# A decoder trunk's down-projection in seven block products instead of eight

## The chip, the core and the metric

The kernel runs on one core of a Trainium2 chip. Its engines work side by side: TensorE (PE, with its weight loads PEld), VectorE (DVE), ScalarE (ACT), GpSimd (POOL) and SyncE (SP), which only issues DMAs here. The metric is the device time of one execution in microseconds. The profile is one execution on the same chip; line numbers such as L650 are lines of the kernel before.

## The reference

One layer over 1024 tokens of 1024 channels, all float32:

```python
h = rms_norm(x, norm_mix_g); z = h @ w_in              # 1024 -> 2048
x = x + concat([pooling(z), diff_attention(z)]) @ w_out
h = rms_norm(x, norm_ffn_g)
gu = h @ ffn_w_in                                      # 1024 -> 2 * 2816
g = causal_depthwise_conv(gu[..., :2816])              # width 3
x = x + (silu(g) * gu[..., 2816:]) @ ffn_w_out         # 2816 -> 1024, the down-projection
return rms_norm(x, norm_final_g)
```

## The kernel before

Every large product is made from float32r parts: an operand is split into a high part (a cast on ACT) and a low part (the difference, on DVE or POOL), and one block takes three matmuls, high by high, high by low and low by high. `split` and `psplit` do it (L78 to L84), `mm3` issues the three.

The stages follow one another. In-projection, attention and pooling (L321 to L511); the output projection in three groups (`out_rows`, L530); then `norm2` and `pair_blocks` (L561 to L600) normalise the rows and build seven transposed operands, b11, b21, b22 and t1 to t4, with high and low parts in 14 buffers of the pool h2. t1 to t4 are sums and differences of row tiles; those of the last pair are made on DVE. The up loop (L689) runs over 22 channel tiles. For each, `up_weights` loads two raw tiles ru and rg (two buffers, tag rw), forms sums sa and sb on POOL and DVE and the high and low parts (uh and ul, sah and sal, and so on), one tile ahead; `ffn_up` makes seven products of 12 matmuls, gathers them in g and cv, applies the convolution, SiLU and gate, and stores cv as 128 rows of `act_rows` in DRAM.

The down-projection (L754) takes the 22 channel tiles in groups of 3, 3, 3, 3, 3, 3 and 4. A group loads and splits its activations (`pair_of`, the low part on DVE) and weights (the low part on POOL). `ffn_down` (L740) goes over 8 row tiles and two column halves: a PSUM bank gets the 9 (or 12) matmuls of the group, and DVE adds it to the row xr of the residual (L750). In the last group `finish` follows each row tile: squares on ACT, a square root, three Newton steps on DVE, the product with the norm's weights, the store.

Instructions are put in order by a scheduler when the program is built; a pool with several buffers makes a new tile wait until the old one in that buffer was last read. Each engine then works in the order given, and so does the SP queue.

## Time and profile before

| | us |
|---|---|
| three runs | 1113.57 to 1114.74, median 1114.7 |
| the profiled execution | 1115.49 |
| its span, first to last instruction | 1113.7 |
| first and last matmul of the down-projection | 857.6 and 1105.8 |

The span is what the trace covers; the profiled execution's own time holds another 1.8 us around it. The up loop's steady part is looked at from 500 to 820, the down-projection's from 885 to 1105.

### The profile page before, as it was taken

How to read it: one execution, taken by the hardware profiler on the slowest of the kernel's cores; microseconds unless marked ns; L12 is line 12 of the kernel's file. 1: busy time of each engine (PE TensorE's matmuls, PEld its weight loads, DVE VectorE, ACT ScalarE, POOL GpSimd, SP SyncE). 2: the span in 40 equal slices, each digit the busy share in tenths (PEclk: the TensorE clock that was granted, in tenths of full speed). 3: DMA queues.
4: the chain of work that ended last, by engine and by line, in shares of the span. 5: the costliest groups of instructions: out<-in, count | busy, mean ns of one | idle time of the engine just before them, and what ended most of it. 6: DMA issues, size and time to landing. Idle time of an engine off the chain costs nothing.

```text
span 1113.7 us, 13597 instructions
## 1 busy us (share of the span) xinstructions
PE 1066.6 (96%) x5011; PEld 884.0 (79%) x5011; DVE 732.3 (66%) x1213; ACT 475.9 (43%) x775; POOL 341.7 (31%) x240
## 2 busy tenths in 40 slices
PE   5999999999899997999999999999999999999997
PEld 4988888887677675878888888888888788888885
DVE  7556787877797689577657656755665655544545
ACT  5557476655752355244333443443344222111133
POOL 3232242433730247133312232221314322221211
PEclk9999999999899998999999999999999999999999
DMA  8010110110386742123122212222247632212112
GB/s 242 28 50 27 43 46 19 43 39 26 133 278 216 242 171 76 57 95 95 57 94 95 93 59 96 90 81 76 82 127 267 223 114 99 89 60 95 39 50 102
DMA packets 85990, 111.76 MB, mean 100 GB/s; under 512 B 3618, under 2 KB 66303, under 8 KB 85924
## 3 DMA queue, kind: packets, MB, share of 16 engines
q1 hardware_dynamic: 79300, 86.78, 24.4%
q10 hardware_dynamic: 6624, 24.12, 5.5%
q8 instruction: 39, 0.64, 0.2%
q14 instruction: 27, 0.22, 0.1%
HBM read 82.57 MB, written 28.32 MB: 100 GB/s over the span
## 4 chain that ended last, share of the span: by engine, by line
PE 81%; DVE 8%; issue 4%; DMA 3%; ACT 1%; POOL 1%; SPq 1%; DVEq 0%; ACTq 0%; POOLq 0%
PE p L650 36%; PE fo L747 7%; PE fo L749 7%; PE fo L748 7%; PE tpa L402 1%; PE z_q L144 1%; PE z_q L145 1%; PE z_q L143 1%; PE o L538 1%; PE o L539 1%; PE o L540 1%; PE z_p L143 1%; PE z_p L144 1%; PE z_p L145 1%; PE z_v L143 1%
## 5 line engine op out<-in xcount | busy, mean ns | idle before, releaser
L747 PE MATMUL fo<-w,a 128*128 128x512 f32 x352 | 137.3, 390 | 2.8 <-DVE xr L750 2.8
L750 DVE TENSOR_TENSOR xr<-xr,fo 128x512 f32<-128x512 f32 x112 | 75.9, 684 | 97.0 <-PE fo L749 96.3
L748 PE MATMUL fo<-w,a 128*128 128x512 f32 x352 | 137.0, 389 | 0.0
L749 PE MATMUL fo<-w,a 128*128 128x512 f32 x352 | 137.0, 389 | 0.0
L80 POOL TENSOR_TENSOR w<-rw,w 128x1024 fp32r<-128x1024 f32 x22 | 61.3, 2796 | 156.4 <-ACT w L79 151.1
L628 POOL TENSOR_TENSOR sa<-rg 128x512 f32<-128x512 f32 x22 | 32.9, 1495 | 209.8 <-DMA rg<-in_ffn_w_in_dram 201.3
L80 POOL TENSOR_TENSOR ul<-ru,uh 128x1024 fp32r<-128x1024 f32 x22 | 58.1, 2642 | 71.8 <-PE p L650 37.6
L747 PEld LDWEIGHTS fo<-w,a 128*128 128x128 f32 x352 | 66.1, 188 | 17.6 <-DVE xr L750 4.0
L749 PEld LDWEIGHTS fo<-w,a 128*128 128x128 f32 x352 | 66.1, 188 | 13.9
L748 PEld LDWEIGHTS fo<-w,a 128*128 128x128 f32 x352 | 66.1, 188 | 13.6
L79 ACT CAST a<-ra 128x1024 fp32r<-128x1024 f32 x22 | 23.1, 1051 | 118.8 <-DVE xr L750 64.1
L362 ACT ACTIVATE p<-p,nm 128x128 f32<-128x128 f32 (+7 forms) x64 | 49.6, 776 | 40.9 <-DVE nm L361 40.5
L650 PE MATMUL p<-t4h,gt 128*128 128x512 f32 x176 | 58.9, 396 | 1.7 <-DVE g L675 1.7
L629 DVE TENSOR_TENSOR sa<-sa,ru 128x512 f32<-128x512 f32 x22 | 39.9, 1814 | 21.1 <-POOL sa L628 21.1
L538 PE MATMUL o<-woh,yh 128*128 128x512 f32 x128 | 51.9, 409 | 1.6 <-DVE x L541 1.4
L349 POOL CAST qz<-q 64x128 fp32r<-64x128 f32 x64 | 24.5, 384 | 92.3 <-PE s L353 85.4
L79 ACT CAST uh<-ru 128x1024 fp32r<-128x1024 f32 x22 | 23.2, 1054 | 68.0 <-PE p L650 67.4
L539 PE MATMUL o<-wol,yh 128*128 128x512 f32 x128 | 50.6, 397 | 1.4 <-POOL wol L80 1.4
L677 DVE TENSOR_TENSOR g<-eb,p 128x512 f32<-128x512 f32 x22 | 15.1, 687 | 55.5 <-PE p L650 55.5
L80 DVE TENSOR_TENSOR a<-ra,a 128x1024 fp32r<-128x1024 f32 x22 | 43.0, 1956 | 12.1 <-ACT a L79 11.6
L540 PE MATMUL o<-woh,yl 128*128 128x512 f32 x128 | 50.0, 393 | 0.9 <-DVE yl L80 0.9
L79 ACT CAST gt<-rg 128x512 fp32r<-128x512 f32 x22 | 13.7, 623 | 82.1 <-PE p L650 75.1
(264 smaller groups left out, 3111.0 us busy)
## 6 DMA issues: line engine op xcount, KB each, us to landing
x_rows<-x ACTq DMA_DIRECT2D x24, 512.0 KB, 3.6
ru<-in_ffn_w_in_dram SPq DMA_DIRECT2D x22, 512.0 KB, 4.0
rg<-in_ffn_w_in_dram SPq DMA_DIRECT2D x22, 512.0 KB, 3.9
act_rows<-cv ACTq DMA_DIRECT2D x22, 512.0 KB, 2.6
rw<-in_ffn_w_out_dram SPq DMA_DIRECT2D x22, 512.0 KB, 4.4
ra<-act_rows SPq DMA_DIRECT2D x22, 512.0 KB, 3.4
x<-in_x_dram SPq DMA_DIRECT2D x16, 512.0 KB, 5.6
x<-x_rows SPq DMA_DIRECT2D x16, 512.0 KB, 3.7
```

Of the source, the lines that this page charges most:

```text
L79: nc.scalar.copy(hi, src)
L80: (lo_eng or nc.gpsimd).tensor_tensor(lo, src, hi.bitcast(F32), op=ALU.subtract)
L362: nc.scalar.activation(s[:, 0:w], s[:, 0:w], AF.Exp, bias=negm[:, c:c + 1], accum_out=sums[:, c:c + 1])
L538: nc.tensor.matmul(ps, yh[:, ts], wh[:, cs], start=n == 0, stop=False)
L539: nc.tensor.matmul(ps, yh[:, ts], wl[:, cs], start=False, stop=False)
L540: nc.tensor.matmul(ps, yl[:, ts], wh[:, cs], start=False, stop=n == len(wo) - 1)
L629: nc.vector.tensor_tensor(s2, s1, a11, op=ALU.subtract)
L650: nc.tensor.matmul(ps, w[:, k, :], h[:, k, :], start=start and k == 0 and n == 0, stop=k == 3 and n == 2, skip_group_check=not start)
L747: nc.tensor.matmul(ps, ah[:, ts], wh[:, cs], start=n == 0, stop=False)
L748: nc.tensor.matmul(ps, ah[:, ts], wl[:, cs], start=False, stop=False)
L749: nc.tensor.matmul(ps, al[:, ts], wh[:, cs], start=False, stop=n == len(ops) - 1)
L750: nc.vector.tensor_tensor(xr[t][:, cs], xr[t][:, cs], ps, op=ALU.add)
```

## The change

The down-projection is made from seven products (Strassen's scheme in Winograd's form) instead of eight. Tokens are cut into halves, channel tiles into even and odd ones, output columns into halves. A product takes 512 tokens, 11 channel pairs and 512 columns, and keeps one PSUM bank for each of its four row tiles over all channels: 4 x 11 x 3 = 132 matmuls. Its banks are then added to one to four blocks of the residual (`ADDS`, `add_product`).

- The seven activation operands are made in the up loop: after each odd tile `store_act` stores three blocks of cv as they are and four sums of two tiles, which POOL forms (sm). `act_rows` becomes seven arrays.
- The weights stay in SBUF as four quarters x, y, z, v of float32 (`load_quarter`, three buffers of h2 each, `wx0` to `wv2`). Four products need differences of quarters; DVE writes them in place (`operands`, L755 of the kernel after).
- Each product goes through six steps of two channel pairs (the last has one). A step loads one activation block, splits it (ah, al) and splits the weights (bh and bl, or b); `al5_2` is product 5, channel pair 2. The order of the products is 1, 2, 5, 7, 6, 3, 4.
- In the last product the top four row tiles are finished beside it; its last three steps are held back and run row tile by row tile.
- In `up_weights` of the second tile a column of the last normalised row is copied into ru and rg before they are loaded.
- cv has three buffers, two small pads are put among the constants, the DMA scratch is 2048.

```diff
-DOWN = [3] * 6 + [4]
+DOWN = (("1", "x", None), ("2", "z", None), ("5", "x", "yx"), ("7", "y", "vy"), ("6", "x", "vx"), ("3", "v", None),
+        ("4", "z", "xz"))
+ADDS = {"1": ((0, 0), (0, 1), (1, 0), (1, 1)), "2": ((0, 0),), "3": ((0, 1),), "4": ((1, 0),), "5": ((0, 1), (1, 1)),
+        "6": ((0, 1), (1, 0), (1, 1)), "7": ((1, 0), (1, 1))}
+STEPS = ((0, 2), (2, 2), (4, 2), (6, 2), (8, 2), (10, 1))
+SCRATCH = 2048
...
+PADS = (8, 8)
...
-    act_d = nc.dram_tensor("act_rows", (FF, S), F32).ap()
+    act_d = nc.dram_tensor("act_rows", (7, FF // 2, 512), F32).ap()
...
+    const.tile([P, PADS[0]], F32, name="pad0")
...
+    const.tile([P, PADS[1]], F32, name="pad1")
...
-        ta = mid.tile([P, S], F32, tag="cv", bufs=2, name=f"ta{j}")
-        tb = mid.tile([P, S], F32, tag="cv", bufs=2, name=f"tb{j}")
+        ta = mid.tile([P, S], F32, tag="cv", bufs=3, name=f"ta{j}")
+        tb = mid.tile([P, S], F32, tag="cv", bufs=3, name=f"tb{j}")
...
+            if ct == 1:
+                nc.vector.tensor_copy(r[:, 0:1], x1[NT - 1][:, D - 1:D])
...
-        cv = mid.tile([P, S], F32, tag="cv", bufs=2, name=f"cv{ct}")
+        cv = cvs[ct] = mid.tile([P, S], F32, tag="cv", bufs=3, name=f"cv{ct}")
...
-        nc.scalar.dma_start(act_d[ct * P:(ct + 1) * P, :], cv)
+        store_act(ct, cv)
+    cvs = {}
+    def op_rows(n, m, count=1):
+        return act_d[n - 1, m * P:(m + count) * P, :].rearrange("(m p) c -> p m c", p=P)
+    def store_act(ct, cv):
+        m = ct // 2
+        if ct % 2 == 0:
+            nc.scalar.dma_start(act_d[0, m * P:(m + 1) * P, :], cv[:, 0:512])
+            return
+        for i, n in enumerate((2, 4)):
+            nc.scalar.dma_start(act_d[n - 1, m * P:(m + 1) * P, :], cv[:, i * 512:i * 512 + 512])
+        a11, a21, a12, a22 = cvs[ct - 1][:, 0:512], cvs[ct - 1][:, 512:1024], cv[:, 0:512], cv[:, 512:1024]
+        sm = [mid.tile([P, S], F32, tag="sm", bufs=2, name=f"sm{m}_{i}") for i in range(2)]
+        s1, s2, s3, s4 = [sm[i // 2][:, (i % 2) * 512:(i % 2) * 512 + 512] for i in range(4)]
+        nc.gpsimd.tensor_tensor(s3, a11, a21, op=ALU.subtract)
+        nc.gpsimd.tensor_tensor(s1, a21, a22, op=ALU.add)
+        nc.gpsimd.tensor_tensor(s2, s1, a11, op=ALU.subtract)
+        nc.gpsimd.tensor_tensor(s4, a12, s2, op=ALU.subtract)
+        for n, t in ((5, s1), (6, s2), (7, s3), (3, s4)):
+            nc.sync.dma_start(act_d[n - 1, m * P:(m + 1) * P, :], t)
...
+    wq = {}
+    def load_quarter(q):
+        b, cs = dict(x=(0, 0), y=(0, 1), z=(1, 0), v=(1, 1))[q]
+        src = ffn_w_out.rearrange("(m b p) c -> b p m c", b=2, p=P)[b][:, :, cs * 512:cs * 512 + 512]
+        wq[q] = [h2.tile([P, 4, 512], F32, tag="h2", name=f"w{q}{i}") for i in range(3)]
+        for m, n in STEPS:
+            nc.sync.dma_start(wq[q][m // 4][:, m % 4:m % 4 + n, :], src[:, m:m + n, :])
+    def quarter(q, m, n):
+        return wq[q][m // 4][:, m % 4:m % 4 + n, :]
+    def operands(gi, m, n):
+        num, q, upd = DOWN[gi]
+        if upd:
+            a, b = upd
+            if q == b:
+                nc.vector.tensor_tensor(quarter(b, m, n), quarter(a, m, n), quarter(b, m, n), op=ALU.subtract)
+        raw = mid.tile([P, 2, 512], F32, tag="rw", bufs=2, name=f"ra{num}_{m}")[:, 0:n, :]
+        nc.sync.dma_start(raw, op_rows(int(num), m, n))
+        if gi == 0:
+            a2 = h2.tile([P, 4, 512], F32R, tag="h2", name=f"a{num}_{m}")
+            ah, al = a2[:, 0:n, :], a2[:, 2:2 + n, :]
+        else:
+            ah = wide.tile([P, 2, 512], F32R, tag="x", bufs=4, name=f"ah{num}_{m}")[:, 0:n, :]
+            al = mid.tile([P, 2, 512], F32R, tag="cv", bufs=3, name=f"al{num}_{m}")[:, 0:n, :]
+        split(ah, al, raw, nc.vector)
+        if m // 2 % 2:
+            b2 = h2.tile([P, 4, 512], F32R, tag="h2", name=f"b{num}_{m}")
+            wh, wl = b2[:, 0:n, :], b2[:, 2:2 + n, :]
+        else:
+            wh = mid.tile([P, 2, 512], F32R, tag="st", bufs=2, name=f"bh{num}_{m}")[:, 0:n, :]
+            pool, tag, bufs = (mid, "sm", 2) if gi else (wide, "x", 4)
+            wl = pool.tile([P, 2, 512], F32R, tag=tag, bufs=bufs, name=f"bl{num}_{m}")[:, 0:n, :]
+        split(wh, wl, quarter(q, m, n))
+        return ah, al, wh, wl
+    def banks(gi):
+        if gi % 2:
+            return [sc_ps(f"fo_{gi}_{j}") for j in range(3)] + [mm_ps(f"fo_{gi}_3")]
+        return ([tp_ps(f"fo_{gi}_{j}").rearrange("p a b -> p (a b)") for j in range(2)]
+                + [mm_ps(f"fo_{gi}_2"), pv_ps(f"fo_{gi}_3")])
+    def tile_part(ps, op, j, m, n):
+        ah, al, wh, wl = op
+        js = slice(j * P, (j + 1) * P)
+        for i in range(n):
+            mm3(ps, ah[:, i, js], al[:, i, js], wh[:, i, :], wl[:, i, :], m + i == 0, m + i == NCT // 2 - 1)
+    def add_product(num, j, ps):
+        for h, c in ADDS[num]:
+            t, cs = 4 * h + j, slice(c * 512, c * 512 + 512)
+            if num == "4":
+                nc.vector.tensor_tensor(xr[t][:, cs], xr[t][:, cs], ps, op=ALU.subtract)
+            else:
+                nc.vector.tensor_tensor(xr[t][:, cs], xr[t][:, cs], ps, op=ALU.add)
+    outs, sums = {}, {}
+    def half_sum(t, half):
+        if t not in outs:
+            outs[t] = h2.tile([P, 4, 512], F32, tag="h2", name=f"o_{t}").rearrange("p a c -> p (a c)")[:, 0:D]
+            sums[t] = small.tile([P, 2], F32, tag="fs", bufs=8, name=f"ss2_{t}")
+        nc.scalar.activation(outs[t][:, 0:512], xr[t][:, half * 512:half * 512 + 512], AF.Square,
+                             accum_out=sums[t][:, half:half + 1])
...
-        if pool_path:
-            nc.scalar.mul(o, xg, r)
+        nc.scalar.mul(o[:, 512:1024], o[:, 512:1024], r)
+        nc.vector.scalar_tensor_tensor(o[:, 0:512], xr[t][:, 0:512], r, g_bc3[:, 0:512], op0=ALU.mult, op1=ALU.mult)
...
+        nc.scalar.dma_start(out[t * P:(t + 1) * P, 512:1024], o[:, 512:1024])
+        nc.sync.dma_start(out[t * P:(t + 1) * P, 0:512], o[:, 0:512])
+    def right_half(t):
+        half_sum(t, 1)
+        nc.gpsimd.tensor_tensor(outs[t][:, 512:1024], xr[t][:, 512:1024], g_bc3[:, 512:1024], op=ALU.mult)
...
+    late = 3
+    for gi, (num, q, upd) in enumerate(DOWN):
+        for c in (q if upd is None else upd):
+            if c not in wq:
+                load_quarter(c)
+        ps = banks(gi)
+        last = gi == len(DOWN) - 1
+        held = []
+        for si, (m, n) in enumerate(STEPS):
+            op = operands(gi, m, n)
+            if last and si >= late:
+                held.append((op, m, n))
+                continue
+            for j in range(4):
+                tile_part(ps[j], op, j, m, n)
+            if gi == 0 and si == 0:
+                load_x1_back()
+            if last and si == 1:
+                for t in range(4):
+                    right_half(t)
+                    half_sum(t, 0)
+                    finish(t)
+                for t in range(4, NT):
+                    right_half(t)
         if gi == 2:
             warm = small.tile([P, 1], F32, tag="warm", bufs=1, name="warm")
             nc.scalar.activation(warm, xr[0][:, 0:1], AF.Sqrt, bias=1.0, scale=0.0)
-        ffn_down(ops, gi, gi == len(DOWN) - 1)
+        for j in range(4):
+            for op, m, n in held:
+                tile_part(ps[j], op, j, m, n)
+            add_product(num, j, ps[j])
+            if last:
+                half_sum(4 + j, 0)
+                finish(4 + j)
...
+    nc = _bacc.Bacc("TRN2", target_bir_lowering=False, num_devices=1, dynamic_dma_scratch_size=SCRATCH)
```

DVE at the last row norm, before (x1_2_7 is the last row tile, ta3 and tb3 hold the last pair's t1, t2 and t4, sbl0 and gt0 belong to the first channel tile):

```order
L577 SCALAR_TENSOR_TENSOR x1_2_7_4419<-x1_2_7_4419,rr_f7_4458,g_ffn_3925 128x1024
L80 TENSOR_TENSOR gt0_4516<-rg0_4504,gt0_4516 128x512
L594 TENSOR_TENSOR ta3_4461<-x1_2_7_4419,x1_2_6_4363 128x512
L80 TENSOR_TENSOR sbl0_4524<-sb0_4507,sbh0_4523 128x1024
L596 TENSOR_TENSOR ta3_4461<-x1_2_7_4419,ta3_4461 128x512
L84 TENSOR_TENSOR t2l_3943<-tp_t2_2_4349,t2h_3936 128x4x128
L84 TENSOR_TENSOR t4l_3945<-tp_t4_2_4356,t4h_3938 128x4x128
L597 TENSOR_TENSOR tb3_4462<-x1_2_6_4363,ta3_4461 128x512
```

DVE at the same place after the change:

```order
L585 SCALAR_TENSOR_TENSOR x1_2_7_4421<-x1_2_7_4421,rr_f7_4460,g_ffn_3927 128x1024
L86 TENSOR_TENSOR gt0_4518<-rg0_4506,gt0_4518 128x512
L602 TENSOR_TENSOR ta3_4463<-x1_2_7_4421,x1_2_6_4365 128x512
L629 COPY ru1_4529<-x1_2_7_4421 128x1
L86 TENSOR_TENSOR sbl0_4526<-sb0_4509,sbh0_4525 128x1024
L629 COPY rg1_4532<-x1_2_7_4421 128x1
L604 TENSOR_TENSOR ta3_4463<-x1_2_7_4421,ta3_4463 128x512
L90 TENSOR_TENSOR t2l_3945<-tp_t2_2_4351,t2h_3938 128x4x128
L90 TENSOR_TENSOR t4l_3947<-tp_t4_2_4358,t4h_3940 128x4x128
L90 TENSOR_TENSOR b22l_3943<-tp_b22_3_4469,b22h_3936 128x4x128
L605 TENSOR_TENSOR tb3_4464<-x1_2_6_4365,ta3_4463 128x512
```

The two copies into ru1 and rg1, on which the loads of the second channel tile's weights wait, stand behind t1 and behind sbl0.

DVE in the down-projection, before (in the fourth group, whose banks fo_3 are added to the rows xr, with the split of an activation tile a15 between):

```order
L750 TENSOR_TENSOR xr_0_7372<-xr_0_7372,fo_3_0_1_8027 128x512
L80 TENSOR_TENSOR a15_8400<-ra15_8398,a15_8400 128x1024
L750 TENSOR_TENSOR xr_1_7375<-xr_1_7375,fo_3_1_0_8038 128x512
L750 TENSOR_TENSOR xr_1_7375<-xr_1_7375,fo_3_1_1_8049 128x512
L750 TENSOR_TENSOR xr_2_7378<-xr_2_7378,fo_3_2_0_8060 128x512
L750 TENSOR_TENSOR xr_2_7378<-xr_2_7378,fo_3_2_1_8071 128x512
L750 TENSOR_TENSOR xr_3_7381<-xr_3_7381,fo_3_3_0_8082 128x512
```

DVE in the down-projection after the change, behind the second product, whose four banks fo_1 are added (al5 are low parts of the third product's activations, wx, wy and wz the weight quarters):

```order
L793 TENSOR_TENSOR xr_0_7513<-xr_0_7513,fo_1_0_7712 128x512
L793 TENSOR_TENSOR xr_1_7516<-xr_1_7516,fo_1_1_7713 128x512
L793 TENSOR_TENSOR xr_2_7519<-xr_2_7519,fo_1_2_7714 128x512
L755 TENSOR_TENSOR wz0_7703<-wx0_7467,wz0_7703 128x1024
L793 TENSOR_TENSOR xr_3_7522<-xr_3_7522,fo_1_3_7715 128x512
L86 TENSOR_TENSOR al5_4_7995<-ra5_4_7992,ah5_4_7994 128x1024
L755 TENSOR_TENSOR wy1_7910<-wv1_8128,wy1_7910 128x1024
L755 TENSOR_TENSOR wx1_7468<-wv1_8128,wx1_7468 128x1024
L755 TENSOR_TENSOR wy1_7910<-wv1_8128,wy1_7910 128x1024
L755 TENSOR_TENSOR wx1_7468<-wv1_8128,wx1_7468 128x1024
L86 TENSOR_TENSOR al5_6_8030<-ra5_6_8027,ah5_6_8029 128x1024
L755 TENSOR_TENSOR wz1_7704<-wx1_7468,wz1_7704 128x1024
```

The updates of the quarters for products 7, 6 and 4 stand between the splits that the third product needs.

POOL in the up loop, before (sa, sb and ul are parts of the weights of tiles 11 and 12):

```order
L628 TENSOR_TENSOR sa11_5821<-rg11_5819 128x512
L631 TENSOR_TENSOR sb11_5822<-ru11_5817,rg11_5819 128x512
L80 TENSOR_TENSOR ul11_5828<-ru11_5817,uh11_5827 128x1024
L628 TENSOR_TENSOR sa12_5950<-rg12_5948 128x512
L631 TENSOR_TENSOR sb12_5951<-ru12_5946,rg12_5948 128x512
L80 TENSOR_TENSOR ul12_5957<-ru12_5946,uh12_5956 128x1024
```

POOL in the up loop after the change (cv8 and cv9 are the results of earlier tiles, sm4 their sums):

```order
L638 TENSOR_TENSOR sa11_5880<-rg11_5878 128x512
L641 TENSOR_TENSOR sb11_5881<-ru11_5876,rg11_5878 128x512
L86 TENSOR_TENSOR ul11_5887<-ru11_5876,uh11_5886 128x1024
L714 TENSOR_TENSOR sm4_1_5867<-cv8_5638 128x512
L638 TENSOR_TENSOR sa12_6009<-rg12_6007 128x512
L641 TENSOR_TENSOR sb12_6010<-ru12_6005,rg12_6007 128x512
L715 TENSOR_TENSOR sm4_0_5866<-cv8_5638,cv9_5767 128x512
L716 TENSOR_TENSOR sm4_0_5866<-sm4_0_5866,cv8_5638 128x512
L717 TENSOR_TENSOR sm4_1_5867<-cv9_5767,sm4_0_5866 128x512
L86 TENSOR_TENSOR ul12_6016<-ru12_6005,uh12_6015 128x1024
```

One sum stands ahead of sa12, three stand between sb12 and ul12.

## Rows read from the trace of the kernel before

**Rows 1.** The page, busy time of TensorE, and its clock in 40 slices.
```profile
PE 1066.6 (96%) x5011; PEld 884.0 (79%) x5011; DVE 732.3 (66%) x1213; ACT 475.9 (43%) x775; POOL 341.7 (31%) x240
...
PEclk9999999999899998999999999999999999999999
```

**Rows 2.** The page, the chain that ended last, by engine.
```profile
PE 81%; DVE 8%; issue 4%; DMA 3%; ACT 1%; POOL 1%; SPq 1%; DVEq 0%; ACTq 0%; POOLq 0%
```

**Rows 3.** Busy time by stretch: us, each engine (instructions), clock, DMA share, GB/s.
```profile
...
480.00:490.00 10.00, 8.26 (x29) 6.32 (x28) 8.12 (x9) 3.82 (x4) 3.53 (x2) 0.83 0.50 156
500.00:820.00 320.00, 320.00 (x1413) 264.81 (x1412) 204.74 (x201) 129.06 (x155) 90.57 (x52) 1.00 0.26 83
858.00:866.00 8.00, 8.00 (x37) 6.62 (x36) 4.28 (x5) 1.38 (x2) 2.97 (x1) 1.00 0.97 360
885.00:1105.00 220.00, 220.00 (x972) 182.15 (x972) 109.78 (x166) 46.83 (x73) 50.82 (x19) 1.00 0.22 77
...
```

**Rows 4.** Waits of PE after 400 us: us in total, times, longest.
```profile
...
PE fo L747 <- DVE xr L750: 2.8, 3, 1.0
PE tp_t L584 <- DVE t2l L84: 2.5, 1, 2.5
...
PE p L650 <- DVE g L675: 1.7, 1, 1.7
...
```

**Rows 5.** Timeline of the SP queue in the down-projection: start us, us, what.
```profile
...
933.15 3.68 SPq L708 DMA_DIRECT2D ra<-act_rows  x2
...
965.79 3.67 SPq L708 DMA_DIRECT2D ra<-act_rows  x2
...
```

**Rows 6.** By tile (fo, sa, ul): ns min/median/max, first and last start us.
```profile
L747 PE MATMUL fo<-w,a x352: 389/389/504, 857.6 to 1105.4; 128*128 128x512 f32 x176
L750 DVE TENSOR_TENSOR xr<-xr,fo x112: 672/686/689, 862.0 to 1106.3; 128x512 f32<-128x512 f32 x112
...
L630 DVE TENSOR_TENSOR sb<-ru,sa x22: 676/693/2305, 428.8 to 820.9; 128x512 f32<-128x512 f32 x22
L80 DVE TENSOR_TENSOR sal<-sa,sah x22: 1211/1226/2109, 431.1 to 824.3; 128x1024 fp32r<-128x1024 f32 x22
...
L80 POOL TENSOR_TENSOR ul<-ru,uh x22: 2354/2631/3160, 422.4 to 819.7; 128x1024 fp32r<-128x1024 f32 x22
```

**Rows 7.** Timeline of DVE and POOL at the last row norm; the last cv.
```profile
438.47 1.21 DVE L80 TENSOR_TENSOR sbl<-sb,sbh 128x1024 fp32r<-128x1024 f32 x1
...
438.73 3.16 POOL L80 TENSOR_TENSOR ul<-ru,uh 128x1024 fp32r<-128x1024 f32 x1 [0.73 <-ACT uh L79]
...
439.61 2.84 DVE L596 TENSOR_TENSOR ta<-x,ta 128x512 f32<-128x512 f32 x1
...
878.67 1.27 DVE L686 TENSOR_TENSOR cv<-cv,p 128x512 f32<-128x512 f32 x2
```

**Rows 8.** Groups by line, 500 to 820: busy us, mean ns, idle before.
```profile
L631 POOL TENSOR_TENSOR sb<-ru,rg 128x512 f32<-128x512 f32 x17 | 21.9, 1289 | 0.0
...
L677 DVE TENSOR_TENSOR g<-eb,p 128x512 f32<-128x512 f32 x17 | 11.7, 687 | 39.8 <-PE p L650 39.8
```

**Rows 9.** Timeline: the sixth tile's low part on POOL, its first matmul on PE.
```profile
537.25 2.42 POOL L80 TENSOR_TENSOR ul<-ru,uh 128x1024 fp32r<-128x1024 f32 x1 [5.29 <-PE p L650]
...
561.99 0.39 PE L650 MATMUL p<-b11h,ul 128*128 128x512 f32 x1
```

**Rows 10.** Groups by line, 880 to 1070.
```profile
...
L80 POOL TENSOR_TENSOR w<-rw,w 128x1024 fp32r<-128x1024 f32 x15 | 41.3, 2763 | 122.0 <-ACT w L79 122.0
L80 DVE TENSOR_TENSOR a<-ra,a 128x1024 fp32r<-128x1024 f32 x15 | 29.9, 1993 | 6.4 <-ACT a L79 6.0
L79 ACT CAST a<-ra 128x1024 fp32r<-128x1024 f32 x15 | 15.8, 1051 | 112.3 <-DVE xr L750 64.1 <-PE fo L749 41.1 <-DMA ra<-act_rows 5.3
...
```

**Rows 11.** Timeline of DVE at the end.
```profile
...
1109.16 1.42 DVE L737 SCALAR_TENSOR_TENSOR o<-xr,rr_l,g_fin 128x512 f32<-128x512 f32 x2
```

**Rows 12.** By tile (p): ns min/median/max of one form.
```profile
...
L650 PE MATMUL p<-b11h,uh x88: 387/389/775, 429.0 to 843.3; 128*128 128x512 f32 x88
...
```

More of the change, by code (lines that the diff above doesn't have):

```diff
@@ L704, in load_x1_back @@
             xr.append(xt)
-    def pair_of(src, name, tag, eng):
-        raw = mid.tile([P, S], F32, tag=tag, bufs=2, name=f"r{name}")
-        nc.sync.dma_start(raw, src)
-        t = h2.tile([P, 2, S], F32R, tag="h2", name=name)
-        split(t[:, 0, :], t[:, 1, :], raw, eng)
-        return t[:, 0, :], t[:, 1, :]
-    def finish(t):
-        o = x_tile(F32, f"o_{t}")
-        pool_path = t % 2 == 0
-        if pool_path:
-            xg = e_tile(F32, f"xg_{t}")
-            nc.gpsimd.tensor_tensor(xg, xr[t], g_bc3, op=ALU.mult)
-        ss = small.tile([P, 2], F32, tag="ss2", name=f"ss2_{t}")
-        for half in range(2):
-            cs = slice(half * 512, half * 512 + 512)
-            nc.scalar.activation(o[:, cs], xr[t][:, cs], AF.Square, accum_out=ss[:, half:half + 1])
+    wq = {}
@@ L723, in finish @@
+    def finish(t):
+        o, ss = outs[t], sums[t]
         var = small.tile([P, 1], F32, tag="var", name=f"varl_{t}")
@@ L730, in finish @@
         r = newton(r, var, f"l{t}")
-        if pool_path:
-            nc.scalar.mul(o, xg, r)
+        nc.scalar.mul(o[:, 512:1024], o[:, 512:1024], r)
+        nc.vector.scalar_tensor_tensor(o[:, 0:512], xr[t][:, 0:512], r, g_bc3[:, 0:512], op0=ALU.mult, op1=ALU.mult)
+        if t < NT - 1:
             nc.sync.dma_start(out[t * P:(t + 1) * P, :], o)
             return
-        for half in range(2):
-            cs = slice(half * 512, half * 512 + 512)
-            nc.vector.scalar_tensor_tensor(o[:, cs], xr[t][:, cs], r, g_bc3[:, cs], op0=ALU.mult, op1=ALU.mult)
-            nc.sync.dma_start(out[t * P:(t + 1) * P, cs], o[:, cs])
-    def ffn_down(ops, gi, last):
-        for t in range(NT):
-            ts = slice(t * P, (t + 1) * P)
-            for half in range(2):
-                cs = slice(half * 512, half * 512 + 512)
-                ps = sc_ps(f"fo_{gi}_{t}_{half}")
-                for n, (ah, al, wh, wl) in enumerate(ops):
-                    nc.tensor.matmul(ps, ah[:, ts], wh[:, cs], start=n == 0, stop=False)
-                    nc.tensor.matmul(ps, ah[:, ts], wl[:, cs], start=False, stop=False)
-                    nc.tensor.matmul(ps, al[:, ts], wh[:, cs], start=False, stop=n == len(ops) - 1)
-                nc.vector.tensor_tensor(xr[t][:, cs], xr[t][:, cs], ps, op=ALU.add)
-            if last:
-                finish(t)
+        nc.scalar.dma_start(out[t * P:(t + 1) * P, 512:1024], o[:, 512:1024])
[3 more added lines that the diff above has]
+        nc.gpsimd.tensor_tensor(outs[t][:, 512:1024], xr[t][:, 512:1024], g_bc3[:, 512:1024], op=ALU.mult)
     g_bc3 = mid.tile([P, D], F32, tag="gt", bufs=1, name="g_fin")
@@ L756, in trunk_kernel @@
     last_w = w_now["3"][0][:, 0, 0:1].bitcast(F32)
-    ct = 0
-    for gi, n in enumerate(DOWN):
-        ops = []
-        for c in range(ct, ct + n):
-            rows = slice(c * P, (c + 1) * P)
-            ops.append(pair_of(act_d[rows, :], f"a{c}", "st", nc.vector)
-                       + pair_of(ffn_w_out[rows, :], f"w{c}", "rw", nc.gpsimd))
-        ct += n
-        if gi == 0:
-            load_x1_back()
+    late = 3
[22 more added lines that the diff above has]
+                    right_half(t)
         if gi == 2:
@@ L811 @@
     from concourse.bass_utils import run_bass_kernel_spmd as _run
-    nc = _bacc.Bacc("TRN2", target_bir_lowering=False, num_devices=1)
+    nc = _bacc.Bacc("TRN2", target_bir_lowering=False, num_devices=1, dynamic_dma_scratch_size=SCRATCH)
     arrays, args = {}, []
```

## The prediction

> **What bounds the kernel now.** First the page's busy shares: TensorE is busy 1066.6 of 1113.7 us, and the granted clock is nine tenths or more in all but two of the 40 slices [rows 1]. A busy PE alone proves little, so second the chain that ended last: 81% of it is PE, 8% DVE [rows 2]. Third the busy time by stage: in the up loop (500 to 820) and in the down-projection (885 to 1105) PE is busy in every microsecond at clock 1.00, while DVE has 64% and 50%, POOL 28% and 23% [rows 3]. There only fewer matmuls, or a new wait of PE, can move the time. Fourth, PE's waits after 400 us, few and named: 2.8 us in three pieces on the eviction L750, 2.5 us on t2l, 1.7 us on g [rows 4].
>
> The price of one matmul comes from the queue's timeline: the activation loads of two successive groups of three channel tiles start at 933.15 and 965.79 [rows 5]. The 32.64 us between them hold 8 x 2 x 9 = 144 matmuls, 0.2267 us each; the 0.389 of a row in [rows 6] overlaps with the next.
>
> **The change part by part.** The sum is made against the profiled execution, 1115.5 us (span 1113.7), which lies 0.8 above the median of 1114.7.
>
> Matmuls. Before: 8 row tiles x 2 halves x 22 channel tiles x 3 = 1056. After: 7 products x 4 row tiles x 11 channel pairs x 3 = 924, in the same form (128x128 stationary, 512 columns moving). The 132 that go lay back to back on PE: 132 x 0.2267 = **-29.9 us**. A stall that would undo this must come from the operands, below.
>
> First evictions. Before, a bank is full after nine matmuls, 2.04 us, and DVE, still busy with the last channel tile, let PE wait three times, 2.8 us in all [rows 4]. A product now keeps four banks for its 132 matmuls and the next one has four others, so no eviction is due there: **-2.8** (at worst 0, if the same DVE work delays a split instead).
>
> The last row norm. Before, POOL's ul (438.73, 3.16 us) ran beside DVE's second difference (L596, 439.61, 2.84 us) [rows 7]; that form takes 0.68 at its fastest [rows 6], and PE then waited 2.5 us for t2l [rows 4]. After, ru1 and rg1 are loaded behind two one-column copies, and so ul1 comes after that difference: up to 2.1 us of the wait go. In return uh1 is later, and two matmuls of the second channel tile stand early in PE's order. Ends: -4 (the wait, and most of it again for a lower clock, as in the stretch at 480 below) and +2 (uh1 takes the place of t2l, for nearly as long). I take **-1.5**, nearest to the 2.1 less two copies and some of uh1.
>
> Up loop. Each pair of channel tiles adds four 512-wide sums on POOL, 1.29 us each [rows 8], and has seven stores of 256 KB for two of 512 KB. POOL is free for 229 of 320 us [rows 3]. Three of the sums wait for the odd tile's cv and stand ahead of an ul in POOL's order. The cover: ul6 started at 537.25 and took 2.42, and its first matmul is at 561.99 [rows 9], 22 us later, while the three sums take 3.9. On SP, the stores stand ahead of raw loads of the next tiles, and wait for the same sums; these loads have the same lead. DVE waited 39.8 us for PE in L677 alone [rows 8], so it can give a sum its turn. DMA has a share of 26% [rows 3]. **0**, and +3 if that cover is gone in places.
>
> First product. Its weights, the x1 rows and the activations come where the queues already had 97%, 360 GB/s (858 to 866) [rows 3], in pieces of 2 KB instead of 4. What would be late is a split of the fourth or fifth step. From 0 to +4 (half of that full stretch); taken **+1**.
>
> Second product. Its first low part, bl2_0, stands on POOL behind three sums of the last pair, which need the last cv, and behind b2_2, b2_6 and b2_10. The last cv ended at 879.94 [rows 7]. The chain is 3 x 1.29 + 1.29 + 3 x 2.35 = 12.2 us at the fastest [rows 6, 8] and 13.4 with 2.76, POOL's mean in this stage [rows 10]: done at 892.2 to 893.4. The first product begins where fo begins now, at 857.6 [rows 6]; with 132 matmuls and 21 of the up loop between them it ends at 857.6 + 153 x 0.2267 = 892.3. From 0 to +4 (the cv itself later); taken **+1**.
>
> The weight updates. Four times a quarter is overwritten by a difference. The order puts 18 pieces of three of them close together on DVE, between al5_0 and al7_0. al5_0 takes the buffer of the third split before it, so it can start 36 matmuls before the second product ends; al7_0 is due when the third one (5) ends: 168 x 0.2267 = 38.1 us. In between lie 21 operations of 1024, four of 512 and four evictions. Evictions read PSUM and never took over 0.689 [rows 6]. With the fastest of the others, 1.21 and 0.68 [rows 6], DVE needs 25.4 + 2.7 + 2.7 = 30.8 us and is 7 early. With the mean of this stage, 1.99 [rows 10], and the half size in proportion, 1.12, it needs 41.8 + 4.5 + 2.7 = 49.0 and is 11 late. Rows 7 show what lies between: DVE's sbl, POOL's ul and DVE's difference, at their fastest 1.21 + 2.35 + 0.68 = 4.2 us one after the other, took from 438.47 to 442.45, 4.0 us. The two engines took turns. So the five splits that POOL has in that stretch (11.8 us, of them 2.7 beside evictions) add 9.1 to DVE's 30.8: 39.9, 2 late. I take **+2**, from the rows where the turns are seen; ends 0 and +11.
>
> [...]
>
> ACT has two casts of 1.05 [rows 10] in each of 35 full steps and two of about 0.6 in each of seven short ones: 82 of 209 us, no bound. In the last product ten squares on ACT and eight products with g on POOL (8 x 1.29 = 10.3) stand ahead of the late steps, which PE needs 72 matmuls, 16.3 us, after its start. From 0 to +3; taken **+1**.
>
> The end. DVE has one of the two multiplies at 1109.16, 1.42 us together [rows 11]; ACT has the other at the same time: **-0.7**. The pads and the smaller DMA scratch add no instruction, and no row prices an address: 0.
>
> Sum: -29.9 - 2.8 - 1.5 + 0 + 1 + 1 + 2 + 1 - 0.7 = -29.9. From 1115.5 that is 1085.6, and 0.8 less for the median: **1085**.
>
> **The rivals.**
> 1. Operand preparation becomes the bound. For it: DVE has 7 x 6.7 us of activation splits and 4 x 6.7 of updates at the fastest, POOL 7 x 13 of weight splits and 10 at the end, together 175 of 209 if they take turns, and more than that locally. Against it: from 500 to 820 DVE and POOL were busy 295 of 320 us together, and PE never waited [rows 3]. With 11 for the updates, 4 for each of the first two products and 3 at the end: 1085 + 9 + 3 + 3 + 2 = 1102.
> 2. Every new wait is covered and the last row norm gives its 4: 1085 - 5 - 2.5 = 1077.5. For it: in the order PE takes the products with high parts first where a low part is late. Against it: the second product's chain, which even at its fastest ends with the first product.
> [...]
>
> [...]
>
> That the change doesn't do what it says can be left out: the order holds 132 matmuls less.
>
> **How the numbers follow.** Forecast 0.70 (its own range 1079 to 1094), rival 1 0.17 (1094 to 1110), rival 2 0.08 (1076 to 1079), rival 3 0.05. The range 1079 to 1099 leaves out rival 2, rival 3 and about half of rival 1, some 2 in 10. About 0.2%, 2.2 us, is what a measurement of this kernel can tell from no change. Faster: 0.70 + 0.17 + 0.08 = 0.95; of rival 3 I put 0.01 near the old time and 0.04 above it.
>
> **What would show it.** The span from the first fo matmul to the last is about 218 us (209.5 of products, 4.8 of the up loop's last matmuls, some 4 of waits) against 248; no wait of PE on an eviction; the difference L604 under 1.3 us and PE's wait on t2l under 1; no PE wait between 500 and 820; waits on al5 and al7 of about 2 us, on bl2_0 of about 1. I am wrong if PE waits for DVE or POOL at most steps of the products, if the granted clock falls there, or if the up loop shows waits on ul or on cv.

## The result, and the profile after

The changed kernel takes 1098.6 us (median of 4 runs, 1097.2 to 1099.9) against 1114.1 (4 runs, 1113.5 to 1114.7): ratio 0.986, 95% interval 0.9843 to 0.9878. The forecast of 1085 had the sign right and is 13.6 us too fast. The time lies 0.4 us inside the upper end of the range of 1079 to 1099, and in the part of it (from 1094 on) that the prediction gave to rival 1.

The page of the changed kernel answers to [rows 1, 2]: TensorE, its clock in 40 slices, and the chain that ended last.

```profile
PE 1046.9 (96%) x4879; PEld 859.2 (78%) x4879; DVE 759.3 (69%) x1203; ACT 509.0 (46%) x819; POOL 466.1 (43%) x308
...
PEclk9999999999999988999999999999999999999998
...
PE 75%; DVE 10%; issue 6%; POOL 4%; DMA 2%; ACT 2%; SPq 1%; POOLq 0%; ACTq 0%; DVEq 0%
```

The 132 matmuls are gone (5011 less 4879), yet PE's busy time fell by only 19.7 us, not by 29.9. PE's part of the chain fell from 81% to 75%, and what took its place is DVE and POOL.

The waits of PE after 400 us (us in total, times, longest), as [rows 4]:

```profile
PE fo L151 <- DVE al L86: 2.7, 1, 2.7
PE fo L150 <- POOL bl L86: 2.0, 1, 2.0
PE p L660 <- DVE g L685: 1.7, 1, 1.7
PE p L660 <- ACT uh L85: 1.5, 1, 1.5
PE tp_t L592 <- DVE t2l L90: 0.9, 1, 0.9
...
PE fo L150 <- POOL b L86: 0.4, 1, 0.4
```

The evictions are gone from the list; al, bl and uh are new in it. Busy time by stretch, as [rows 3]:

```profile
480.00:490.00 10.00, 8.34 (x37) 6.54 (x36) 9.57 (x10) 5.07 (x6) 7.44 (x4) 1.00 0.25 78
500.00:820.00 320.00, 320.00 (x1400) 262.48 (x1399) 205.83 (x200) 126.74 (x152) 138.95 (x84) 1.00 0.33 106
890.00:900.00 10.00, 8.18 (x36) 6.28 (x34) 3.52 (x2) 1.97 (x3) 9.92 (x5) 1.00 0.60 178
930.00:940.00 10.00, 7.30 (x33) 5.66 (x32) 9.85 (x8) 2.96 (x4) 3.05 (x1) 1.00 0.48 158
940.00:950.00 10.00, 10.00 (x39) 8.03 (x38) 10.00 (x9) 2.14 (x4) 3.37 (x1) 0.83 0.49 159
```

Two things are to be seen. The wait on al in 930 to 940 is followed by a stretch with a granted clock of 0.83, in a part of it (940.4 to 943.8) of 0.50: 39 matmuls, where ten microseconds hold 44 at 0.229. And from 500 to 820, where PE works without a pause at clock 1.00 in both kernels and its instructions are the same, it did 1400 matmuls where it did 1413 [rows 3]. Each one had become slower. It begins early: the same 69 matmuls of the first projections, first and last, in the kernel before and then in the changed one:

```profile
46.43 0.40 PE L145 MATMUL z_q<-hTh,wlo_q 128*128 128x512 f32 x1
...
61.85 0.39 PE L145 MATMUL z_v<-hTh,wlo_v 128*128 128x512 f32 x1
```

```profile
45.30 0.40 PE L151 MATMUL z_q<-hTh,wlo_q 128*128 128x512 f32 x1
...
61.16 0.40 PE L151 MATMUL z_v<-hTh,wlo_v 128*128 128x512 f32 x1
```

The 68 steps took 15.42 us, 0.2268 each, and now 15.86, 0.2332 each. The duration in the row does not show it; the distance of the starts does. ACT's 1024-wide cast of uh takes the same time in both (mean 1054 and 1050 ns), so not everything became slower.

### The profile page after: what moved, and what is told of

Same layout as the page of the kernel before. It is cut to its first block, busy times and chain, and to the rows that moved or that the text cites. A ratio compares the mean times of both kernels' runs of the same rounds, so it can differ in the third digit from the quotient of the medians.

```text
span 1096.1 us, 13535 instructions
## 1 busy us (share of the span) xinstructions
PE 1046.9 (96%) x4879; PEld 859.2 (78%) x4879; DVE 759.3 (69%) x1203; ACT 509.0 (46%) x819; POOL 466.1 (43%) x308
## 4 chain that ended last, share of the span: by engine, by line
PE 75%; DVE 10%; issue 6%; POOL 4%; DMA 2%; ACT 2%; SPq 1%; POOLq 0%; ACTq 0%; DVEq 0%
PE p L660 36%; PE fo L151 4%; PE fo L150 4%; PE fo L149 4%; PE o L546 1%; PE o L547 1%; PE o L548 1%; PE tpa L410 1%; PE z_q L150 1%; PE z_q L151 1%; PE z_q L149 1%; POOL b L86 1%; PE z_p L149 1%; PE z_p L150 1%; PE z_p L151 1%
## 5 line engine op out<-in xcount | busy, mean ns | idle before, releaser
L86 DVE TENSOR_TENSOR al<-ra,ah 128x1024 fp32r<-128x1024 f32 (+1 forms) x36 | 64.9, 1808 | 55.8 <-PE fo L151 25.5
L85 ACT CAST ah<-ra 128x1024 fp32r<-128x1024 f32 (+1 forms) x36 | 35.1, 977 | 70.2 <-DMA ra<-act_rows 56.2
L357 POOL CAST qz<-q 64x128 fp32r<-64x128 f32 x64 | 26.9, 422 | 92.3 <-PE s L361 85.5
L150 PE MATMUL fo<-bl,ah 128*128 128x512 f32 x144 | 56.2, 390 | 2.0 <-POOL bl L86 2.0
L85 ACT CAST uh<-ru 128x1024 fp32r<-128x1024 f32 x22 | 23.1, 1050 | 73.9 <-PE p L660 67.4
L149 PE MATMUL fo<-bh,ah 128*128 128x512 f32 x144 | 56.5, 392 | 0.0
L151 PE MATMUL fo<-bh,al 128*128 128x512 f32 x144 | 56.2, 391 | 0.0
L151 PE MATMUL fo<-b,al 128*128 128x512 f32 x120 | 47.4, 399 | 2.7 <-DVE al L86 2.7
L687 DVE TENSOR_TENSOR g<-eb,p 128x512 f32<-128x512 f32 x22 | 15.1, 686 | 49.5 <-PE p L660 49.5
L150 PE MATMUL fo<-b,ah 128*128 128x512 f32 x120 | 47.7, 397 | 0.4 <-POOL b L86 0.4
L149 PE MATMUL fo<-b,ah 128*128 128x512 f32 x120 | 47.3, 398 | 0.0
L685 DVE TENSOR_TENSOR g<-eb,p 128x512 f32<-128x512 f32 x22 | 15.0, 682 | 42.7 <-ACT eb L684 42.7
L549 DVE TENSOR_TENSOR x<-x,o 128x512 f32<-128x512 f32 x48 | 32.5, 682 | 17.4 <-PE o L548 17.1
```

What stands on the lines that cost most here:

```text
L85: nc.scalar.copy(hi, src)
L86: (lo_eng or nc.gpsimd).tensor_tensor(lo, src, hi.bitcast(F32), op=ALU.subtract)
L149: nc.tensor.matmul(ps, wh, hh, start=first, stop=False)
L150: nc.tensor.matmul(ps, wh, hl, start=False, stop=False)
L151: nc.tensor.matmul(ps, wl, hh, start=False, stop=last)
L549: nc.vector.tensor_tensor(xt[:, cs], xt[:, cs], ps, op=ALU.add)
```

## The experiments

"Without pads" is run 1; the runs 6 to 10 and 12 build on it. Times are medians of 4 to 6 runs, ratios are to the kernel before on the same chip (1113.2 to 1113.6).

**1, e1_no_pads.**
```
-    const.tile([P, PADS[0]], F32, name="pad0")
-    const.tile([P, PADS[1]], F32, name="pad1")
```


> The changed kernel without its two pads: every tile behind them lies 32 or 64 bytes lower, and the order of the instructions is the same. In the changed kernel a 512-column matmul follows the one before after 0.2333 us in the stage of the projections and 0.2289 in the up loop, in the kernel before after 0.2267 at its commonest in both; every other engine's operation has the same duration in both. Theory A (addresses: the pads cost it): the step goes back to 0.2267 in the up loop and below 0.230 in the projections, and the time falls by 6 to 10 us, to 1089 to 1093. Theory B (more traffic: the sums, the stores, the splits): the step stays at 0.229, the time at 1097 to 1100. Theory C (the chip of that run): the step is 0.229 here and in a kernel before of the same chip.

1091.75 us, ratio 0.9812 (0.979 to 0.9834), outside the interval of the changed kernel. The same 69 matmuls go from 45.90 to 61.32, 0.2268 a step, and the up loop does 1412:

```profile
500.00:820.00 320.00, 320.00 (x1412) 264.75 (x1411) 208.62 (x203) 129.20 (x156) 141.15 (x86) 1.00 0.33 105
```

POOL and DMA are as busy there as with the pads (141 us, 0.33), so traffic (theory B) is out: the pads cost 6.9 us by the medians, 5.3 by the ratios.

**2, e2_before_pads.** The same two lines put into the kernel before.

> The kernel before with the two pads alone, no other change: the same instructions at addresses that are 32 or 64 bytes higher, as far as they lie behind the pads. Theory A (the pads cost each matmul): the step of the up loop rises from 0.2267 to about 0.229, that of the projections to about 0.233, and the time rises by 6 to 11 us, to 1120 to 1125. Theories B (traffic) and C (the chip): 1113 to 1115, and a step of 0.2267.

1118.83 us, ratio 1.005 (1.0034 to 1.0066). The 69 matmuls go from 46.02 to 61.88 (0.2332), and the up loop does 1399. In the down-projection from 890 to 1105 us nothing changes; the third row is the kernel before:

```profile
500.00:820.00 320.00, 320.00 (x1399) 262.49 (x1398) 203.12 (x200) 126.84 (x153) 89.75 (x49) 1.00 0.26 83
890.00:1105.00 215.00, 215.00 (x950) 178.05 (x949) 107.59 (x159) 45.27 (x68) 48.48 (x19) 1.00 0.22 78
```

```profile
890.00:1105.00 215.00, 215.00 (x950) 178.01 (x950) 107.75 (x164) 46.83 (x73) 50.82 (x19) 1.00 0.22 79
```

Two tiles that nothing reads make the kernel before 5.6 us slower, a little less than expected, since the step of the down-projection stays. Its two operands are both tiles of h2, the pool that also holds the moving operands of the up loop. This pool lies at the lower end of SBUF and moved with the pads; the stationary operands of the up loop lie at the upper end (pool wide, side="right") and did not. B and C fall, A stands.

**3, e3_no_updates.**
```
-            if q == b:
-                nc.vector.tensor_tensor(quarter(b, m, n), quarter(a, m, n), quarter(b, m, n), op=ALU.subtract)
```


> The changed kernel without the weight updates: the products 5, 7, 6 and 4 take the plain quarter where the product needs the difference. My theory (the burst of updates on DVE delays one low part, and the wait of 2.7 us costs clock besides: 0.83 in the ten microseconds behind it): that wait and the fall go, 1098.6 less 4 to 5, so 1093 to 1095. Rival (the wait is one of a chain, and POOL's low parts are late next): a wait of PE on bl takes its place, 1096 to 1099.

1093.78 us, ratio 0.9824 (0.9804 to 0.9844): 4.8 less by the medians and 4.0 by the ratios, whose intervals just touch. PE does not wait for al any more; bl2_0 stays (2.4). How the wait came about stands in the changed kernel's timeline of DVE (the operations before al5_2):

```profile
926.45 1.23 DVE L86 TENSOR_TENSOR al<-ra,ah 128x1024 fp32r<-128x1024 f32 x1 [2.96 <-ACT ah L85]
930.15 1.23 DVE L755 TENSOR_TENSOR wy<-wv,wy 128x1024 f32<-128x1024 f32 x1 [2.48 <-DMA wv<-in_ffn_w_out_dram]
931.29 3.47 DVE L755 TENSOR_TENSOR wx<-wv,wx 128x1024 f32<-128x1024 f32 x1
934.68 1.21 DVE L755 TENSOR_TENSOR wy<-wv,wy 128x1024 f32<-128x1024 f32 x1
935.82 1.21 DVE L755 TENSOR_TENSOR wx<-wv,wx 128x1024 f32<-128x1024 f32 x1
936.95 1.21 DVE L755 TENSOR_TENSOR wz<-wx,wz 128x1024 f32<-128x1024 f32 x1
938.09 1.21 DVE L86 TENSOR_TENSOR al<-ra,ah 128x1024 fp32r<-128x1024 f32 x1
```

DVE stood idle for 2.48 us at an update whose quarter v was not loaded, with the split al5_2 behind it, and then did five updates first. The second of them took 3.47 us instead of 1.2, while POOL had a low part of 3.05 us from 930.62 on.

**4, e4_no_copies.**
```
-            if ct == 1:
-                nc.vector.tensor_copy(r[:, 0:1], x1[NT - 1][:, D - 1:D])
```


> The changed kernel without the two one-column copies that hold back the second up weight load. The prediction said that they give 1.5 us (ends 4 and -2). In the trace of the changed kernel PE waits 0.9 us for t2l where it waited 2.5, but 1.5 us for uh1 where it did not wait. If the two cancel: 1097.5 to 1099.5. If the copies give what the prediction said: 1100 or more, with a wait of 2.5 us on t2l. If they cost: under 1097.5.

1097.05 us, ratio 0.9853 (0.9833 to 0.9871). The time is 0.5 under the band for "the two cancel", but it is not told apart from the changed kernel: neither a gain of the copies nor a cost is shown. The wait on t2l is back,

```profile
PE tp_t L592 <- DVE t2l L90: 2.5, 1, 2.5
```

and that on uh is gone. In the changed kernel the timeline shows the exchange:

```profile
440.38 0.14 DVE L629 COPY ru<-x 128x1 f32<-128x1 f32 x1
...
440.65 0.38 SPq L631 DMA_DIRECT2D ru<-in_ffn_w_in_dram  x1
...
441.64 0.68 DVE L604 TENSOR_TENSOR ta<-x,ta 128x512 f32<-128x512 f32 x1
...
444.67 1.04 ACT L85 CAST uh<-ru 128x1024 fp32r<-128x1024 f32 x1 [4.57 <-DMA ru<-in_ffn_w_in_dram]
```

The difference takes 0.68 instead of 2.84 [rows 7], and uh waits 4 us for the load that the copy held back.

**5, e5_all_shifted.** In the changed kernel, with its pads:
```
+    rpad = ctx.enter_context(tc.tile_pool(name="rpad", bufs=1, side="right"))
+    rpad.tile([P, 16], F32, name="pad2")
```


> The changed kernel with its pads and 64 bytes more at the other end of SBUF, so that the tiles there move down by 64 bytes too; the order of the instructions is the same. Divided by 128, the addresses of both operands of a matmul leave 96 in the kernel before and in the one without pads; with the pads one operand leaves 32 and the other 96; here both leave 32. Theory R (only the difference between the two operands counts): the step goes back to 0.2267 us in the up loop, and the time to 1090 to 1094. Theory S (32 is the costly place, whichever operand lies there, and the stationary operand costs more): the step is 0.233 or more in the up loop and the projections, and the time 1103 to 1125.

1106.12 us, ratio 0.9943 (0.9921 to 0.9965). The 69 matmuls go from 46.58 to 62.44 (0.2332), and the up loop does 1373 (0.233):

```profile
500.00:820.00 320.00, 320.00 (x1373) 257.59 (x1372) 201.33 (x197) 124.17 (x149) 141.68 (x84) 1.00 0.32 104
```

R, as it was put, falls: an equal remainder by 128 does not help. The numbers of S came out, but run 2 speaks against it: in its down-projection both operands leave 32, and the step is what it was without the pads. The last section has a reading that fits both. In the changed kernel the stationary operand lies at 32 in the projections (0.2332) and the moving one in the up loop (0.229).

**6, e6_tail.**
```
+        if t in (5, 6):
+            nc.gpsimd.tensor_scalar(o[:, 512:1024], o[:, 512:1024], r, None, op0=ALU.mult)
+        else:
             nc.scalar.mul(o[:, 512:1024], o[:, 512:1024], r)
```


> The changed kernel without pads; besides, the last product with 1/rms of the right halves of the row tiles 5 and 6 is made by POOL in place of ACT. In the trace without pads the root sd of row tile 7 stands on ACT behind those two products, and the end comes 9.0 us after the last matmul, 7.5 in the kernel before. My theory (that queue is the cause): the end comes 7.6 to 8.2 us after the last matmul, and the time is 0.8 to 1.4 us lower than without pads, 1090.4 to 1091 where that has 1091.75. Rival (the DVE chain of the rows 5 and 6 or the stores end last): 8.7 to 9.2 us, no change.

1092.63 us, ratio 0.9824 (0.9808 to 0.984): no gain. In the changed kernel, ACT's part of the end was this (o of row 5 and 6, then sd, o and the store of row 7):

```profile
1088.65 0.72 ACT L814 ACTIVATE o<-o,rr_l 128x512 f32<-128x512 f32 x1
...
1089.71 0.72 ACT L814 ACTIVATE o<-o,rr_l 128x512 f32<-128x512 f32 x1 [0.34 <-DVE rr_l L117]
...
1090.34 0.19 ACT L810 ACTIVATE sd<-varl 128x1 f32<-128x1 f32 x1
...
1091.56 0.72 ACT L814 ACTIVATE o<-o,rr_l 128x512 f32<-128x512 f32 x1 [1.03 <-DVE rr_l L117]
...
1092.31 0.38 ACTq L819 DMA_DIRECT2D out_dram<-o  x1
```

In the run, sd no longer waits for a product, but POOL takes 3.65 us for the two, and the 512 KB of row 6 are now the last store:

```profile
1082.16 3.65 POOL L812 TENSOR_SCALAR o<-o,rr_l 128x512 f32<-128x512 f32 x2 [10.14 <-DVE rt_l L114]
...
1085.56 0.33 SPq L820 DMA_DIRECT2D out_dram<-o  x1
1085.99 0.41 SPq L817 DMA_DIRECT2D out_dram<-o  x1
```

The queue on ACT is the cause of sd's delay; what the end would be without it this edit did not show, because it made a store late.

**7, e7_second_start.**
```
-        if m // 2 % 2:
+        if m // 2 % 2 != (gi == 1):
```


> The changed kernel without pads; besides, the second product takes the buffers of its low parts the other way round: its first low part goes into a tile that is free early, and the second one into the buffer that waits for the sums of the last pair. Without pads PE waits 3.1 us for bl2_0, and the eight matmuls after it run at half the clock, some 1.6 us more. My theory (the buffer and the place on POOL behind the sums are the cause): no wait at the start of the second product, and 3 to 5 us less, 1087 to 1089. Rival (the low parts of the steps after it are late instead): a wait of 1 to 3 us on bl2_2 or bl2_6, 1089.5 to 1092.

1095.04 us, ratio 0.984 (0.9819 to 0.9862), which overlaps the interval of run 1. Between 880 and 1070 the wait on bl is gone, and al has taken more than its place:

```profile
PE fo L150 <- DVE al L85: 6.4, 3, 3.9
```

The cause is right and the gain is not there: with PE 3 us earlier, al2_6, behind the 16 evictions and five updates on DVE (897.5 to 913.1), is what is late. That was neither theory's wait.

**8, e8_updates_later.**
```
+                if num == "7":
+                    v1 = quarter("v", m, 1)[:, 0, 0:1]
+                    first = held_al[{0: 2, 1: 6, 2: 8}[m // 4]][:, 0, 0:1].bitcast(F32)
+                    nc.vector.scalar_tensor_tensor(v1, first, 0.0, v1, op0=ALU.mult, op1=ALU.add)
...
+        if num == "5":
+            held_al[m] = al
```


> The changed kernel without pads; besides, six operations of one column put the updates that need the quarter v behind the activation splits al5_2, al5_6 and al5_8 on DVE; what is computed is the same. Without pads DVE stands idle for 3 us at 923, at an update that waits for the load of v, with al5_2 behind it in its order; then come five updates, and PE waits 2.0 and 0.8 us for al. My theory (the order, not the amount of the updates): both waits go and with them the fall of the clock behind them, 3 to 4 us less, 1087.5 to 1089.5. Rival (DVE has too much to do there in any order, at some 2 us an operation beside POOL): a wait of 1 to 4 us on al5_6, al5_8 or al7_0, 1090 to 1094.

1093.74 us, ratio 0.983 (0.9811 to 0.9849). No wait on al is left; bl has a second one, 1.9 us at 958:

```profile
PE fo L149 <- POOL bl L85: 5.1, 2, 3.1
```

The time is the one that the rival gave, but the wait is on a low part of the weights, from POOL, not on one of the activations as the rival had it.

**9, e9_both_orders.** The edits of 7 and 8, and for product 5:
```
+    behind = {("5", 4): ("2", 6), ("5", 6): ("2", 6), ("5", 8): ("2", 8), ("5", 10): ("2", 8),
...
+                    w1 = quarter(a, m, 1)[:, 0, 0:1]
```


> The changed kernel without pads, with the two edits of the last runs together (buffers of the second product's low parts the other way round; updates that need the quarter v behind al5_2, al5_6 and al5_8), and one more: the updates of x that the product 5 needs stand behind al2_6 and al2_8. With either edit alone the time did not fall: the waits of PE on bl2_0 and al5 went, and others came, 3.9 us on al2_6 and 1.6 on al5 with the first, 1.9 on a low part at 958 us with the second. My theory (each wait is a matter of the order on DVE and POOL, and all can be had away together): at most 2 us of waits between 885 and 1060, no fall of the clock there, 1085 to 1089. Rival (the two engines together have too much work between 885 and 960 in any order): 3 to 6 us of waits again, on whatever stands last, 1090 to 1094.

1091.85 us, ratio 0.9808 (0.9791 to 0.9826), the same as without pads. PE waits 4.3 us for bl and 1.5 for al: the rival is right. POOL's timeline, with two low parts in the first row:

```profile
930.36 17.14 POOL L85 TENSOR_TENSOR bl<-wx,bh 128x1024 fp32r<-128x1024 f32 x2 [6.39 <-ACT bh L84]
948.45 10.61 POOL L85 TENSOR_TENSOR bl<-wy,bh 128x1024 fp32r<-128x1024 f32 x1 [0.95 <-ACT bh L84]
```

From 930 to 956.8 us DVE had no pause; its 1024-wide operations of two SBUF inputs took 1.2 us each. Of the pairs of one-column operations that this edit put between them, the first took 0.2 us and two took 2.4:

```profile
926.75 0.22 DVE L758 SCALAR_TENSOR_TENSOR wv<-al,wv 128x1 f32<-128x1 f32 x2
...
937.17 2.38 DVE L758 SCALAR_TENSOR_TENSOR wv<-al,wv 128x1 f32<-128x1 f32 x2
...
945.15 2.44 DVE L758 SCALAR_TENSOR_TENSOR wv<-al,wv 128x1 f32<-128x1 f32 x2
```

The last pair ends where POOL's two low parts end (947.5), and a low part took 2.44 us without the updates (run 3, the last row below). So the two seem to have run there, and to have waited for the rest of their 17.14 us. The low part of product 7 took 8.26 us in the changed kernel, and 2.44 in run 3, without the updates (a row of each):

```profile
955.67 8.26 POOL L86 TENSOR_TENSOR bl<-wy,bh 128x1024 fp32r<-128x1024 f32 x1 [11.16 <-ACT bh L85]
```

```profile
948.78 2.44 POOL L86 TENSOR_TENSOR bl<-wy,bh 128x1024 fp32r<-128x1024 f32 x1 [10.23 <-ACT bh L85]
```

**10, e10_no_copies_too.** Run 9 with the edit of run 4.

> As the run before, and without the two one-column copies at the second channel tile. If the copies' gain on t2l is given back on uh1, as the run without them showed, 0 to 1.5 us below the run before; if they gain without the pads, above it.

1091.64 us, ratio 0.9807 (0.9787 to 0.9827): no difference from run 9, as in run 4 against the changed kernel.

**11, e11_at_0_and_64.** Without pads, and
```
+    rpad.tile([P, 8], F32, name="pad2")
...
+    const.tile([P, 8], F32, name="pad1")
```


> The changed kernel without its pads, and 32 bytes more at either end of SBUF: the order is the same, and the addresses of the tiles that lay at 96 (divided by 128) are at 0 at the lower end and at 64 at the upper. In the up loop the moving operand lies at 0 and the stationary at 64, in the projections the other way round. If only 32 is a costly place: 0.2267 in both stages and 1090 to 1094. If 64-byte boundaries are better than 96: below 0.2267 and below 1088. If 96 alone is free: 0.229 or more in one stage or both, 1095 to 1115, and the stage tells which operand.

1096.6 us, ratio 0.9851 (0.9834 to 0.9868). The 69 matmuls go from 46.81 to 62.68 (0.2334), and the up loop does 1399:

```profile
500.00:820.00 320.00, 320.00 (x1399) 262.79 (x1399) 206.42 (x200) 126.81 (x153) 139.08 (x83) 1.00 0.32 104
```

The first two theories fall. The third, that 96 alone is free, has its numbers here, the time and both steps; but the down-projection of run 2 has both operands at 32 and is free. The steps are those of the changed kernel, though every remainder is another. What the two runs share is that the lower end has moved by 64 bytes against the upper.

**12, e12_second_start_no_updates.** Run 7 with the edit of run 3.

> The changed kernel without pads, with the low parts of the second product the other way round, and without the weight updates (products 5, 7, 6 and 4 take the plain quarter): the run is there to show where the time is. In the run with both orders, four low parts of POOL in a row took 2.7, 17.1 (two together) and 10.6 us between 921 and 959 us while DVE ran updates and splits one after the other at 1.2 us each; without the updates such a low part took 2.4. My theory (the updates of DVE hold POOL up, and with the pads they are all that the forecast missed beside the tail): waits of PE between 885 and 1060 under 1.5 us, and 1084 to 1087. Rival (the 16 evictions of the first product hold up al2_6 in any case): 2 to 4 us of wait there, 1088 to 1091.

1083.73 us, ratio 0.9734 (0.9721 to 0.9747). From 885 to 1065 PE is busy in 179.4 of 180 us at clock 1.00, and no low part on POOL between 914 and 950 took more than 3.2 us:

```profile
885.00:1065.00 180.00, 179.37 (x792) 148.20 (x791) 99.33 (x115) 73.24 (x100) 100.99 (x45) 1.00 0.41 137
```

My theory stands: with pads and updates away, the time is where the forecast was. The eight microseconds from run 1 (1091.75) to here are what the updates and the second start together cost. The evictions alone hold nothing up.

Run 1 is the shortest kernel that computes the whole, beside 9 and 10 that equal it: 1.9% under the kernel before, 0.6% under the changed one by the medians.

## Why the prediction was right in sign and 13.6 us short

- **Matmuls, -29.9: right for those that went.** What failed is the sentence "The pads and the smaller DMA scratch add no instruction, and no row prices an address: 0". The pads move the tiles at the lower end of SBUF against those at the upper, and in the projections and the up loop, whose matmuls take one operand from each end, a matmul pays 2 to 7 ns (runs 1, 2, 5 and 11). Over the whole kernel that gave back 5 to 7 us. An unpriced effect needs bounds on both sides, and this term got none.
- **First evictions, -2.8: right.** No wait of PE on one is left.
- **Last row norm, -1.5: 0 measured.** The t2l wait went from 2.5 to 0.9, as said, and uh1 took its place with 1.5. Of the ends given it was between the two.
- **Up loop, 0: right on waits.** POOL rose from 91 to 139 us there [rows 3] and PE never waited; the slower step is the pads'.
- **First product, +1: 0 measured.** No wait; the stretch from 858 to 866 had a DMA share of 0.21, where it was 0.97 [rows 3].
- **Second product's start, +1: 2.0 measured** (3.1 without pads, where PE comes earlier), within the ends.
- **Weight updates, +2: mis-sized.** The wait on al is 2.7 us, and eight steps behind it took 0.43 us in place of 0.23, at a granted clock of 0.50 (940.4 to 943.8). From 885 to 1085 the clock is 0.99: rival 3, slower than before by the clock, did not come. Removed alone the updates give 4.0 to 4.8 us (run 3), and together with the second start 8.0 (run 12 against run 1). The working added POOL's time to DVE's, as if they took turns as in [rows 7]. That fits 931.29 in the changed kernel, where DVE's update took 3.47 us in place of 1.2 beside POOL's 3.05 (run 3). Later it mostly doesn't: where DVE had no pause its 1024-wide operations kept their 1.2 us, and a low part of POOL took 8 to 11 in place of 2.44 (8.26 at 955.67 in the changed kernel, 11.37 in run 8, 10.61 in run 9). What decides between the two is not shown. So the delay falls on bl as soon as it is taken from al (5.1 us in run 8, 4.3 in run 9), and no order of those tried gave it back. The part of rival 1 that says "operand preparation becomes the bound" holds from 885 to 960 us; its 1102 was too much.
- **Last product, +1: 0.4 of wait on b and one step of 0.34 us behind it.** Within the ends.
- **The end, -0.7: wrong in sign.** From the start of the last matmul to the end of the span it is 9.4 us (1086.75 to 1096.13) against 7.9. I had counted the shorter last multiply and not that ACT has the same products of the rows 5 and 6 in its queue ahead of the root of row 7. Run 6 shows that this delays the root; that it makes the end later is not shown.

Added up, as an estimate: 5 to 7 for the pads, 8 instead of 3 for the updates and the second start, 2.2 for the end and 1.5 for the row norm, less 1 for the first product. That is 13 to 15, against the 13.6 that the forecast fell short. That the time still lies inside the range is luck as far as the pads go: without them it is 1091.75, in the forecast's own part, and the range had no room set aside for them. Run 12 comes to 1083.7 without the updates and with the other buffers at the second start; the forecast less its 3 for these two would be 1082.

The signs that I named came out as said for the evictions, L604 (0.68), t2l (0.9), 500 to 820 and al5; first to last fo is 225.0 us, not 218.

The traces show operations of one engine that became longer beside the other's: in run 9 two of POOL's low parts took 17.14 us in place of twice 2.44, and at 931.29 in the changed kernel an update of DVE took 3.47 in place of 1.2. In the rows of run 9 POOL's low parts seem to have run at DVE's one-column operations (2.38 us at 937.17 and 2.44 at 945.15, in place of 0.22) and in its pause behind 956.8, not between the 1024-wide operations, which kept their 1.2; at 931.29 and in [rows 7] it was an operation of DVE that became longer (3.47, and 2.84 in place of 0.68).

## What to carry to other kernels

When the same instructions on a saturated TensorE take longer, count the matmuls in a stretch without waits or measure the distance of their starts; then look at where the operands lie in SBUF, since a tile that nothing reads can move one operand against the other (here 2 to 7 ns a matmul). Before moving a wait away from DVE, look at what POOL does beside it: where both prepare operands, count the work of the two together; here, where DVE had no pause, its wide operations kept their 1.2 us and POOL's low parts took 8 to 11 in place of 2.44. At an end that is a chain of small steps, read each engine's whole queue, not only the steps of the last row.
